# Three block pairs by seven products in the second half of the SSD output projection, and norm roots and inverse denominators spread through DRAM

## Chip, cores, metric

The kernel runs on one core of a Trainium2 chip. The metric is the device time of one execution in microseconds (us). Engines are named as in the profile: PE (TensorE matmul), PEld (its weight loads), DVE (VectorE), ACT (ScalarE), POOL (GpSimd), SP (SyncE, which only issues transfers here).

## The reference

One layer of a hybrid decoder in fp32 on 512 tokens of width 1024. Two branches, dilated window attention and a Mamba-2 scan (SSD), are merged by gates; a gated FFN follows.

```
proj = rmsnorm(h) @ w_in                          # q k v z xBC dt gates
q, k, v, z, xbc, dt, gates = split(proj)
# SSD: 32 heads of 64 in 4 groups, chunks of 128
yg = (scan(silu(conv(xbc)), dt) + d_skip*xh) * silu(z)      # 512 x 2048
yg = yg * rsqrt(mean(yg*yg over each group of 512) + eps)   # one root per token and group
ssm = yg * ssm_norm_w
# attention: 24 heads in 3 dilated groups, 8 outputs of 64
attn = sum over groups of softmax(lse) * o        # the denominators are divided out
merged = g0 * (attn @ w_attn_branch) + g1 * (ssm @ w_ssm_branch)
h = h + merged @ w_out
h = h + (silu(gate) * up) @ w_ffn_out             # gate, up = rmsnorm(h) @ w_ffn_in
out = rmsnorm(h)
```

The change is in `ssm @ w_ssm_branch` (2048 by 1024), in the root of each group, and in the division by the denominators.

## The kernel before

All activations are kept transposed, 128 features on the partitions and 512 tokens along the row. To keep fp32 accuracy each operand of a product is split in two parts, hi (ACT copies it to a rounded type, L81 and L258) and lo (DVE subtracts, L82 and L259), and PE multiplies hi by hi, hi by lo and lo by hi (`mm`, L179). One block of 128 outputs over 1024 inputs is thus 8 x 3 = 24 matmuls of 512 columns (`project`).

`Weights` brings the weight blocks in the order of a plan: SP loads a block of 128x1024 into `wraw` (L65) two blocks ahead, ACT and DVE split it into `whi` and `wlo` one block ahead, in three buffers each. One such ring, `wst`, serves all stages up to the FFN. SP's queue is in order, so a load that waits for a buffer holds all behind it.

The stages, by the profile's clock: norm and first values to about 40 us; the SSD projections and the scan in 16 pairs of heads (four per group) to 374; values of group 1 to 395.6 and of group 2 to 417.4; the second half of the SSD output projection to 461; attention to about 673; gates, merge and `w_out` to about 790; FFN to the end. The first half of the SSD output projection (input tiles 0 to 7) follows the third group. `hook` is called between products and lets the pieces of small work, generators that end each piece with `yield`, advance by one. In the SSD stage and in attention a scheduler sets the order on each engine; in the FFN the order on PE is that of the code.

`group_end` (L601) ends a group: `mean_pow` forms the root `gnr` (128x4: token p of chunk c) on POOL (L273), `spread` turns it with four transposes on PE (`turn`, L182) into a row of 512 tokens on all partitions, ACT copies that to `gnb` (L606), and DVE multiplies four tiles by it (L610), which are then split into `ssmh` and `ssml`. `softmax_pair` ends with the inverse denominators `rd` (L814, L815): POOL widens them to `rdw` (L817), four transposes turn them, DVE multiplies `ot` by the result (L824).

`Pairs` serves the FFN: it takes two 128-row blocks of outputs over two halves of inputs as a 2 by 2 block product and computes it by seven products instead of eight. `fa` and `fb` are the raw loads, `fA`, `fS` and `fD` the split blocks and sums of blocks (`first`, `sums13`, `sums24`, `last`). Each product is 4 x 3 = 12 matmuls of 256 columns, 84 in a pair. There the lo part of `fA` and `fD` is completed by an accumulating transfer that POOL issues (L121). In the diff, `w_ssm[j][:, 8:16]` is the block of weights of output block j and input tiles 8 to 15.

Of the kernel before, what the change touches and what calls it, by code (L numbers as in the profile page):

```python
# [14 lines left out]
P = 128  # L15
S = 512
# [78 lines left out]
class Pairs:  # L95

    def __init__(self, nc, wp, fw, pairs):
        self.nc, self.wp, self.fw, self.pairs = nc, wp, fw, pairs  # L100
        self.raw, self.sums, self.left = {}, {}, {}
# [49 lines left out]
    def sums24(self, n):  # L151
        if n >= len(self.pairs):
            return
        r1, r2 = self.raw[n]
        t = self.fw.tile([P, KD * P], F32, tag="s24", name=f"s24_{n}")
        self.nc.vector.tensor_add(t[:, :S], self.sums.pop(n)[:, :S], r1[:, :S])
# [12 lines left out]
def trunk(ctx: ExitStack, tc: tile.TileContext, xT, w_in, w_v, w_dt, w_attn, w_ssm, w_out, w_fi, w_fo,  # L169
# [40 lines left out]

    wst = Weights(nc, wp, _chunk_plan(w_in, w_v, w_attn, w_ssm, w_out))

# [24 lines left out]

    def project(ps, rhs, first=True, last=True, at=None, w=wst):
        h, l, kt = w.next()
# [12 lines left out]
        return ps  # L252
# [85 lines left out]
    relw = [drm.tile([HEADS, LREL[g]], F32, name=f"relw{g}") for g in range(3)]  # L338
    la_d = drm.tile([NSH, S], F32, name="la_d")
    h1_d = drm.tile([P, KD, S], F32, name="h1_d")  # L340
    v_d = [drm.tile([S, S], F32, name=f"v_d{g}") for g in range(3)]
# [196 lines left out]
    with tc.tile_pool(name="sp", bufs=1, reuse_waits="tile") as sp:  # L538
# [62 lines left out]
        def group_end(g):  # L601
            r = mean_pow(sp, [yg.pop((g, "s"))], 512, 4.0 * EPS, "gn")
            yield
            pb = spread(r)
            rb = sp.tile([P, S], F32, tag="gnb", name=f"gnb{g}")
            act.activation(rb, pb, AF.Copy)  # L606
            yield
# [8 lines left out]

        def ssm_half(j, half):
            ps = project(bank("mm"), [ssm[8 * half + i] for i in range(8)])
            if half == 0:
                sbr[j] = sbrp.tile([P, S], F32, tag=f"sbr{j}", name=f"sbr{j}")  # L620
                act.activation(sbr[j], ps, AF.Copy)
            else:
                ev.tensor_add(sbr[j], sbr[j], ps)

# [23 lines left out]
        for g in range(NG):  # L648
# [29 lines left out]
            if g == 2:  # L678
                for j in range(KD):
                    ssm_half(j, 0)  # L680
        pv = [bank("mm") for _ in range(NCH)]
# [14 lines left out]


    attn = [None] * 4
    mscr = [drm.tile([S, 2], F32, name=f"mscr{i}") for i in range(4)]
    nscr = [drm.tile([S, 2], F32, name=f"nscr{i}") for i in range(4)]  # L700
    dscr = [drm.tile([S, 2], F32, name=f"dscr{i}") for i in range(4)]
    ahl_cm = tc.tile_pool(name="ahl", bufs=1, reuse_waits="tile", side="right")

    with tc.tile_pool(name="ap", bufs=1, reuse_waits="tile") as ap:
# [12 lines left out]
        def softmax_pair(hp, q, k):  # L717
# [97 lines left out]
            ev.reciprocal(rd, rd)  # L815
# [8 lines left out]
            ev.tensor_mul(t, t, pr)  # L824
            dump(f"attn{hp}", t)
            attn[hp] = split(holder["ahl"], t, "at", hp)
            yield

# [4 lines left out]

        nc.sync.dma_start(vt[0], v_t[0])
        nc.sync.dma_start(vt[1], by_class(1))
        pv = [bank("mm") for _ in range(NCH)]

        def stage2(tt):
            if tt % 2 == 0:
                vs[0] = tl([P, 2 * S], "P1", f"vs2_{tt}", 2)  # L840
            act.activation(vs[0][:, (tt % 2) * S : (tt % 2) * S + S], pv[tt], AF.Copy)
            if tt % 2:
                nc.sync.dma_start(v_t[2][:, tt - 1 : tt + 1, :], vs[0].rearrange("p (c d) -> p c d", c=2))

        for c in range(4):
            values(pv, 2, c, xn, stage2)
        nc.sync.dma_start(vt[2], by_class(2))
        for j in range(KD):
            ssm_half(j, 1)
            dump(f"sbr{j}", sbr[j])  # L850
        ssm_cm.__exit__(None, None, None)
        holder["ahl"] = ahl_cm.__enter__()
# [46 lines left out]
        for hp in range(4):  # L899
            q, k = [], []  # L900
            for g in range(3):
                ps = project(bank("mm"), xn)
# [29 lines left out]

    HS = S // 2
    fr_cm = tc.tile_pool(name="fr", bufs=1, reuse_waits="tile", side="right")
# [67 lines left out]
    rb2h = fp.tile([P, S], F32, name="rb2h")  # L1002
    half = [slice(0, HS), slice(HS, S)]

# [199 lines left out]
def _chunk_plan(w_in, w_v, w_attn, w_ssm, w_out):  # L1204
    plan = [w_v[0, c] for c in range(4)]
    for g in range(NG):
# [3 lines left out]
        if g == 2:  # L1210
            plan += [w_ssm[j][:, 0:8] for j in range(KD)]
    plan += [w_v[g, c] for g in (1, 2) for c in range(4)]
    plan += [w_ssm[j][:, 8:16] for j in range(KD)]
    for hp in range(4):
# [3 lines left out]
    for j in range(KD):  # L1218
        plan += [w_in[G0 + j], w_attn[j]]
    return plan + [w_out[j] for j in OUT_ORDER]  # L1220

# [89 lines left out]
```

## Time and profile before

| | |
|---|---|
| runs | 1148.74, 1148.74, 1149.55 us, median 1148.74 |
| profiled execution | 1150.79 us, its span 1149.0 |
| granted clock | 0.996 of full speed |
| busy share | PE 99%, PEld 84%, DVE 62%, ACT 50%, POOL 16% |
| instructions | 17104, of them 6636 matmuls |
| DMA | 142.35 MB, mean 124 GB/s |

The profile shows one execution. A row of a timeline gives the start, the duration, the engine, the line, and what is written from what, with the shape; "x4" puts four following ones together; in brackets stands how long the engine had been idle and what ended that. A row of waits gives total time, times and the longest. A row of groups gives the total and the mean duration of one in nanoseconds. Matmuls overlap, so the mean duration of one is longer than the distance from one to the next. A row of transfers gives count, size of one, and the median time from issue to landing.

### The profile page before, as it was taken

How to read it: one execution, taken by the hardware profiler on the slowest of the kernel's cores; microseconds unless marked ns; L12 is line 12 of the kernel's file. 1: busy time of each engine (PE TensorE's matmuls, PEld its weight loads, DVE VectorE, ACT ScalarE, POOL GpSimd, SP SyncE). 2: the span in 40 equal slices, each digit the busy share in tenths (PEclk: the TensorE clock that was granted, in tenths of full speed). 3: DMA queues.
4: the chain of work that ended last, by engine and by line, in shares of the span. 5: the costliest groups of instructions: out<-in, count | busy, mean ns of one | idle time of the engine just before them, and what ended most of it. 6: DMA issues, size and time to landing. Idle time of an engine off the chain costs nothing.

```text
span 1149.0 us, 17104 instructions
## 1 busy us (share of the span) xinstructions
PE 1132.8 (99%) x6636; PEld 969.5 (84%) x6636; DVE 715.3 (62%) x1253; ACT 569.9 (50%) x997; POOL 181.6 (16%) x169
## 2 busy tenths in 40 slices
PE   9999999999999999999999999999999999999996
PEld 6777888878888788888888888888999999988886
DVE  5777897873579333455564534478888777773222
ACT  5555565554345331336536533356767667663321
POOL 3214313222013300011211100000111111100001
PEclk9999999999999999999999999999999999999999
DMA  6343333233332373332333224345688888844322
GB/s 220 130 149 98 121 94 111 92 111 110 92 92 74 110 256 96 106 93 75 93 85 83 63 90 123 112 151 171 148 184 186 191 193 186 172 129 129 101 65 74
DMA packets 51521, 142.35 MB, mean 124 GB/s; under 512 B 6439, under 2 KB 13119, under 8 KB 51184
## 3 DMA queue, kind: packets, MB, share of 16 engines
q1 hardware_dynamic: 42096, 120.90, 33.9%
q0 software_dynamic: 6896, 16.04, 8.4%
q10 hardware_dynamic: 2448, 4.32, 1.3%
q8 instruction: 52, 0.85, 0.3%
q14 instruction: 29, 0.24, 0.1%
HBM read 133.76 MB, written 7.48 MB: 123 GB/s over the span
## 4 chain that ended last, share of the span: by engine, by line
PE 91%; DVE 4%; DMA 2%; ACT 1%; issue 1%; POOL 0%; SPq 0%; ACTq 0%; DVEq 0%; POOLq 0%
PE mm L179 74%; PE aux L179 15%; PE aux L182 2%; DVE wlo L82 1%; DMA x<-xT 0%; DMA lab<-la_d 0%; DVE frl L950 0%; DMA h_d<-h 0%; ACT whi L81 0%; DVE fS_lo L138 0%; DMA fa<-w_fi 0%; DVE xm L469 0%; DVE h L958 0%; POOL n2r L273 0%; DVE fA_lo L131 0%
## 5 line engine op out<-in xcount | busy, mean ns | idle before, releaser
L82 DVE TENSOR_TENSOR wlo<-wraw,whi 128x1024 fp32r<-128x1024 f32 (+2 forms) x156 | 185.7, 1195 | 185.3 <-ACT whi L81 185.1
L81 ACT ACTIVATE whi<-wraw 128x1024 fp32r<-128x1024 f32 (+2 forms) x156 | 152.2, 981 | 267.1 <-PE mm L179 238.1
L179 PE MATMUL mm<-xnh,whi 128*128 128x512 f32 x640 | 251.8, 393 | 1.4 <-DVE acc L530 1.3
L179 PE MATMUL mm<-xnh,wlo 128*128 128x512 f32 x640 | 252.6, 395 | 0.0
L179 PE MATMUL mm<-xnl,whi 128*128 128x512 f32 x640 | 251.1, 392 | 0.0
L179 PEld LDWEIGHTS mm<-xnh,whi 128*128 128x128 f32 x640 | 120.3, 188 | 27.3 <-ACT ce L562 1.7
L179 PEld LDWEIGHTS mm<-xnh,wlo 128*128 128x128 f32 x640 | 120.2, 188 | 26.9 <-issue 2.7
L179 PEld LDWEIGHTS mm<-xnl,whi 128*128 128x128 f32 x640 | 120.2, 188 | 24.9 <-issue 1.2
L179 PE MATMUL mm<-hhl,whi 128*128 128x512 f32 (+1 forms) x171 | 62.6, 366 | 0.6 <-DVE hhl L259 0.6
L179 PE MATMUL mm<-hhh,whi 128*128 128x512 f32 (+1 forms) x171 | 62.8, 368 | 0.2 <-ACT hhh L258 0.2
L179 PE MATMUL mm<-hhh,wlo 128*128 128x512 f32 (+1 forms) x171 | 62.3, 365 | 0.0
L121 POOL DMA_DIRECT2D fD_lo<-w_fi x22 | 19.1, 866 | 246.3 <-DVE h L958 135.8
L563 POOL TENSOR_TENSOR ce<-ce,Cf 128x768 f32<-128x768 f32 x16 | 34.7, 2173 | 140.9 <-ACT ce L562 78.2
L530 DVE SCALAR_TENSOR_TENSOR acc<-mm,hcw,acc 128x511 f32<-128x511 f32 (+2 forms) x72 | 53.2, 743 | 1.0
L138 DVE TENSOR_TENSOR fS_lo<-s,fS_hi 128x1024 fp32r<-128x1024 f32 x44 | 52.0, 1217 | 0.0
L179 PE MATMUL mm<-ssml,whi 128*128 128x512 f32 x128 | 50.2, 392 | 0.0
L179 PE MATMUL mm<-ssmh,wlo 128*128 128x512 f32 x128 | 50.1, 392 | 0.0
L179 PE MATMUL mm<-ssmh,whi 128*128 128x512 f32 x128 | 49.9, 390 | 0.0
L179 PE MATMUL mm<-frh,fS_hi 128*128 128x256 f32 x176 | 49.4, 281 | 0.5 <-ACT c L1031 0.5
L179 PE MATMUL aux<-frh,fS_hi 128*128 128x256 f32 x176 | 49.4, 280 | 0.0
L179 PE MATMUL aux<-frl,fS_hi 128*128 128x256 f32 x176 | 49.1, 279 | 0.0
L179 PE MATMUL aux<-frh,fS_lo 128*128 128x256 f32 x176 | 49.1, 279 | 0.0
(320 smaller groups left out, 2571.1 us busy)
## 6 DMA issues: line engine op xcount, KB each, us to landing
wraw<-w_in SPq DMA_DIRECT2D x80, 512.0 KB, 3.6
fb<-w_fi SPq DMA_DIRECT2D x22, 512.0 KB, 3.7
fa<-w_fi SPq DMA_DIRECT2D x22, 512.0 KB, 5.0
fA_lo<-w_fi POOLq DMA_DIRECT2D x19, 512.0 KB, 5.8
lab<-la_d SPq DMA_DIRECT2D x16, 512.0 KB, 3.7
wraw<-w_ssm SPq DMA_DIRECT2D x16, 512.0 KB, 3.8
wraw<-w_fo SPq DMA_DIRECT2D x15, 512.0 KB, 3.6
wraw<-w_v SPq DMA_DIRECT2D x11, 512.0 KB, 3.7
```

What stands on the lines that cost most here:

```text
L81: self.nc.scalar.activation(hi[:, cs], r[:, cs], AF.Copy)
L82: self.nc.vector.tensor_sub(lo[:, cs], r[:, cs], hi[:, cs])
L121: self.nc.gpsimd.dma_start(lo.rearrange("p (k n) -> p k n", n=P), src, accum_op=ALU.add)
L138: self.nc.vector.tensor_sub(lo, t, hi)
L179: pe.matmul(out, lhsT, rhs, start=start, stop=stop, skip_group_check=True)
L182: pe.transpose(out, src, ident)
L530: ev.scalar_tensor_tensor(acc[:, d:], ps[:, : S - d], hcw[:, t * 4 + 3 - d : t * 4 + 4 - d], acc[:, d:], op0=ALU.mult, op1=ALU.add)
L563: gp.tensor_mul(ce, ce, Cf[:, P:].unsqueeze(1).to_broadcast([P, 2, S - P]))
```

## The change

Three parts. First, in the second half of the SSD output projection, output blocks 0 and 1 stay as they are, and blocks 2 to 7 are computed as three pairs by `seven`, with the class `Rights` forming the sums of the other factor (`mh`, `ml` in the rows). The sums for the first pair are made beside the values of group 2. The weights of these six blocks leave the ring, which ends there; a second ring `wst2` serves what follows, and its first block comes in eight pieces. The last pair's `fD` is split by ACT and DVE, with no accumulating transfer. Second, the roots of groups 0 to 2 and, third, the inverse denominators are written to DRAM and read back to all partitions. Besides, `hook` is called after each of the four value tiles instead of after every second one, values of group 2 leave in four transfers, and `vt` is loaded in the first attention pair.

```diff
-    def last(self, n):
+    def last(self, n, add=True):
         hi, lo = self.parts(self.wp, "w%s", f"fD{n}")
-        self.added(hi[:, :S], lo[:, :S], self.raw.pop(n)[1][:, S:], self.pairs[n][1][:, 4:8])
+        raw = self.raw.pop(n)[1][:, S:]
+        if add:
+            self.added(hi[:, :S], lo[:, :S], raw, self.pairs[n][1][:, 4:8])
+        else:
+            self.nc.scalar.activation(hi[:, :S], raw, AF.Copy)
+            self.nc.vector.tensor_sub(lo[:, :S], raw, hi[:, :S])
...
             if at is not None:
                 if (c, tt) in at:
                     at[c, tt]()
-            elif tt % 2:
+            else:
                 hook(tt == 3)
...
         def group_end(g):
             r = mean_pow(sp, [yg.pop((g, "s"))], 512, 4.0 * EPS, "gn")
-            yield
-            pb = spread(r)
+            if g < 3:
+                nc.sync.dma_start(gn_d[g].rearrange("(c p) -> p c", p=P), r)
+            yield
             rb = sp.tile([P, S], F32, tag="gnb", name=f"gnb{g}")
-            act.activation(rb, pb, AF.Copy)
+            if g < 3:
+                nc.sync.dma_start(rb, gn_d[g : g + 1, :].partition_broadcast(P)[:, 0, :])
+            else:
+                act.activation(rb, spread(r), AF.Copy)
             yield
...
+    class Rights:
+        def whole(self, i):
+            x = self.pool.tile([P, S], F32, tag="mx", name=f"mx{i}", bufs=3)
+            ev.tensor_add(x, self.tiles[i][0], self.tiles[i][1])
+            self.both = x
+            return [x[:, c] for c in half]
+        def parts(self, p, f, sl):
+            hi, lo = self.own[p]
+            act.activation(hi[:, sl, :], f, AF.Copy)
+            ev.tensor_sub(lo[:, sl, :], f, hi[:, sl, :])
+        def upper(self, p):
...
+        def lower(self, p):
...
+    def seven(pool, fi, x, top, bottom, ahead):
+        for n in range(N):
+            if n == N - 1:
+                ahead()
+            r, q, s_ = bank("mm")[:, :HS], bank()[:, :HS], bank()[:, :HS]
+            add_product(r, fi, n, "a11", x.block(True, 0), True, False)
+            c1 = copied(r, "c1", n)
+            fi.first(n + 1)
+            add_product(q, fi, n, "s1", x.mixed(0), True, False)
+            c5 = copied(q, "c5", n)
+            fi.last(n, n < N - 1)
+            add_product(s_, fi, n, "a12", x.block(False, 0), True, True)
+            top(n, 0, s_, c1)
+            fi.sums13(n + 1)
+            add_product(r, fi, n, "s2", x.mixed(1), False, False)
+            u2 = copied(r, "u2", n)
+            if before:
+                finish(*before)
+            add_product(q, fi, n, "s4", x.block(False, 1), False, True)
+            top(n, 1, q, u2)
+            fi.load(n + 2)
+            fi.sums24(n + 1)
+            add_product(r, fi, n, "s3", x.mixed(3), False, False)
+            bottom(n, 1, r, c5)
+            before = n, r
+        finish(*before)
...
+        fs = Pairs(nc, wp, ts, [(w_ssm[j][:, 8:16], w_ssm[j + 1][:, 8:16]) for j in range(2, KD, 2)], True)
+        xs = Rights(ts, ssm[8:])
+        fs.load(0)
+        for p in range(4):
+            xs.upper(p)
...
+        for c in range(4):
+            values(pv, 2, c, xn, stage2)
...
+        for j in range(2):
+            ps = project(bank("mm"), ssm[8:])
+            ev.tensor_add(sbr[j], sbr[j], ps)
+        drain()
+        del quick[:]
+        main[0] = wst2
+        with tc.manual_schedule(engines={mybir.EngineType.PE}):
+            seven(ts, fs, xs, ssm_top, ssm_bottom, lambda: wst2.fill(1))
...
-            rdw = tl([P, NCH, P], "ot", f"rdw_{hp}", 2)
-            gp.tensor_copy(rdw.rearrange("p b (e d) -> p b e d", e=2), rd.unsqueeze(3).to_broadcast([P, NCH, 2, 64]))
-            pr = bank()
-            for b in range(4):
-                turn(pr[:, b * P : b * P + P], rdw[:, b])
+            for e in range(2):
+                nc.sync.dma_start(rscr[hp][e].rearrange("(b p) -> p b", p=P), rd[:, :, e])
             t = tl([P, S], "ot", f"ot{hp}", 2)
             act.activation(perm(t), regular(o1), AF.Copy)
             ev.tensor_add(t, t, o0)
-            ev.tensor_mul(t, t, pr)
+            yield
+            rdw = tl([P, S], "rdw", f"rdw_{hp}", 1)
+            for e in range(2):
+                nc.sync.dma_start(rdw[halves[e], :], rscr[hp][e : e + 1, :].partition_broadcast(64)[:, 0, :])
+            ev.tensor_mul(t, t, rdw)
```

Where the instructions stand, at three places. On PE, at the start of the third direct block of the projection before, every row is 512 wide:

```order
L179 MATMUL mm_3811<-ssmh_151_3604,wlo_3783 128x512
L179 MATMUL mm_3843<-ssmh_108_2625,whi_3814 128x512
L179 MATMUL mm_3843<-ssml_108_2626,whi_3814 128x512
L179 MATMUL mm_3843<-ssmh_108_2625,wlo_3815 128x512
L179 MATMUL mm_3843<-ssmh_109_2630,whi_3814 128x512
```

In the changed kernel, at the start of the second direct block (`mm_3881`), the narrow rows of the first pair appear (`fA`, `fS` its weights, `mh`, `ml` the sums of the other factor):

```order
L185 MATMUL mm_3881<-ssmh_105_2614,whi_3839 128x512
L185 MATMUL mm_3881<-ssml_105_2615,whi_3839 128x512
L185 MATMUL mm_3909<-ssmh_105_2614,fA_hi 128x256
L185 MATMUL mm_3909<-ssml_105_2615,fA_hi 128x256
L185 MATMUL mm_3909<-ssmh_105_2614,fA_lo 128x256
```

So the pair's first product (and its second, 24 narrow matmuls in all) stands ahead of the rest of the second direct block, whose other 22 wide matmuls follow them.

On DVE, after the root of group 0 before (`a`, `cbm` and `acc` are steps of the next pair of heads, `wlo` a weight split):

```order
L560 TENSOR_TENSOR a_1391<-a_1391,cbm_1245 128x1024
L560 TENSOR_TENSOR a_1528<-a_1528,cbm_1245 128x1024
L82 TENSOR_TENSOR wlo_1511<-wraw_1440,whi_1510 128x1024
L530 SCALAR_TENSOR_TENSOR acc_1427<-mm_1370,hcw,acc_1427 128x511
L530 SCALAR_TENSOR_TENSOR acc_1427<-mm_1370,hcw,acc_1427 128x510
L610 SCALAR_TENSOR_TENSOR yg_801<-yg_801,prm,gnb_1276 128x512
```

and in the changed kernel:

```order
L570 TENSOR_TENSOR a_1388<-a_1388,cbm_1247 128x1024
L570 TENSOR_TENSOR a_1525<-a_1525,cbm_1247 128x1024
L562 TENSOR_TENSOR xw_1386<-xtm_1306,te 128x384
L82 TENSOR_TENSOR wlo_1508<-wraw_1437,whi_1507 128x1024
L624 SCALAR_TENSOR_TENSOR yg_802<-yg_802,prm,gnb_1273 128x512
```

The products with `gnb` stand at nearly the same place; the two `acc` went behind them and `xw` came ahead.

On SP before, at the root of group 0, only weight loads follow one another:

```order
L65 DMA wraw_1508<-w_in 128x1024
L65 DMA wraw_1577<-w_in 128x1024
L65 DMA wraw_1646<-w_in 128x1024
L65 DMA wraw_1715<-w_in 128x1024
L65 DMA wraw_1784<-w_in 128x1024
```

and in the changed kernel:

```order
L65 DMA wraw_1505<-w_in 128x1024
L65 DMA wraw_1574<-w_in 128x1024
L614 DMA gn_d<-gnr_1235 128x4x1
L618 DMA gnb_1273<-gn_d 128x512
L65 DMA wraw_1643<-w_in 128x1024
```

The write of the root, which waits for POOL, and the read, which waits for the write to land, stand ahead of the third weight load.

More of the change, by code (lines that the diff above doesn't have):

```diff
@@ L209, in par @@
         return prm[:, a + i : a + i + w]
-    wst = Weights(nc, wp, _chunk_plan(w_in, w_v, w_attn, w_ssm, w_out))
+    plan, rest = _chunk_plan(w_in, w_v, w_attn, w_ssm, w_out)
+    wst = Weights(nc, wp, plan)
+    wst2 = Weights(nc, wp, rest)
+    main = [wst]
     late, quick, slow = [], [], []
@@ L236, in drain, with project @@
             hook(True)
-    def project(ps, rhs, first=True, last=True, at=None, w=wst):
-        h, l, kt = w.next()
+    def project(ps, rhs, first=True, last=True, at=None, w=None):
+        h, l, kt = (w or main[0]).next()
         for k in range(kt):
@@ L339, in trunk @@
     la_d = drm.tile([NSH, S], F32, name="la_d")
+    gn_d = drm.tile([3, S], F32, name="gn_d")
     h1_d = drm.tile([P, KD, S], F32, name="h1_d")
@@ L615, in group_end, with ssm_half @@
                     yield
[L617 to L623, printed above, removed]
+        def ssm_half(j):
+            ps = project(bank("mm"), ssm[:8])
+            sbr[j] = sbrp.tile([P, S], F32, tag=f"sbr{j}", name=f"sbr{j}")
+            act.activation(sbr[j], ps, AF.Copy)
         def transposed(src, tag, bufs, name, t=None):
@@ new lines, in seven, with copied, finish @@
+    def seven(pool, fi, x, top, bottom, ahead):
+        def copied(ps, tag, n):
+            t = pool.tile([P, HS], F32, tag=tag, name=f"{tag}_{n}", bufs=1)
+            act.activation(t, ps, AF.Copy)
+            return t
+        def finish(n, r):
+            add_product(r, fi, n, "a22", x.mixed(2), False, True)
+            bottom(n, 0, r, None)
+        N = len(fi.pairs)
+        before = None
+        for n in range(N):
[23 more added lines that the diff above has]
+        finish(*before)
@@ new lines, in trunk, with lowers, stage2, ssm_top @@
+    with tc.tile_pool(name="ts", bufs=1, reuse_waits="tile") as ts:
+        fs = Pairs(nc, wp, ts, [(w_ssm[j][:, 8:16], w_ssm[j + 1][:, 8:16]) for j in range(2, KD, 2)], True)
+        xs = Rights(ts, ssm[8:])
+        fs.load(0)
+        for p in range(4):
+            xs.upper(p)
+        fs.first(0, add=False)
+        fs.sums13(0)
+        fs.sums24(0)
+        def lowers():
+            for p in range(4):
+                for _ in range(4):
+                    yield
+                xs.lower(p)
+            fs.load(1)
+        quick.append([lowers()])
+        pv = [bank("mm") for _ in range(NCH)]
+        def stage2(tt):
+            t = ts.tile([P, S], F32, tag="vs", name=f"vs2_{tt}", bufs=2)
+            act.activation(t, pv[tt], AF.Copy)
+            nc.sync.dma_start(v_t[2][:, tt, :], t)
+        for c in range(4):
+            values(pv, 2, c, xn, stage2)
+        def ssm_top(n, h, ps, c):
+            o = sbr[2 * n + 2][:, half[h]]
+            ev.tensor_add(o, o, c)
+            ev.tensor_add(o, o, ps)
+        def ssm_bottom(n, h, ps, c):
+            o = sbr[2 * n + 3][:, half[h]]
+            if c is not None:
+                ev.tensor_sub(o, o, c)
+            ev.tensor_sub(o, o, ps)
+        for j in range(2):
[6 more added lines that the diff above has]
+            seven(ts, fs, xs, ssm_top, ssm_bottom, lambda: wst2.fill(1))
+        for j in range(KD):
+            dump(f"sbr{j}", sbr[j])
@@ L698, in trunk @@
+    ssm_cm.__exit__(None, None, None)
     attn = [None] * 4
@@ L700, in trunk @@
     nscr = [drm.tile([S, 2], F32, name=f"nscr{i}") for i in range(4)]
+    rscr = [drm.tile([2, S], F32, name=f"rscr{i}") for i in range(4)]
     dscr = [drm.tile([S, 2], F32, name=f"dscr{i}") for i in range(4)]
@@ L1211, in _chunk_plan @@
             plan += [w_ssm[j][:, 0:8] for j in range(KD)]
-    plan += [w_v[g, c] for g in (1, 2) for c in range(4)]
-    plan += [w_ssm[j][:, 8:16] for j in range(KD)]
+    head = plan + [w_v[g, c] for g in (1, 2) for c in range(4)] + [w_ssm[j][:, 8:16] for j in range(2)]
+    plan = []
     for hp in range(4):
```

66 lines of the change are left out of this document (42 added, 24 removed).

## The prediction

> **What bounds the kernel now.** I read the page first, for the engine that is never idle and for the chain that ended last.
>
> ```profile
> span 1149.0 us, 17104 instructions
> ...
> PE 1132.8 (99%) x6636; PEld 969.5 (84%) x6636; DVE 715.3 (62%) x1253; ACT 569.9 (50%) x997; POOL 181.6 (16%) x169
> ...
> PEclk9999999999999999999999999999999999999999
> ...
> PE 91%; DVE 4%; DMA 2%; ACT 1%; issue 1%; POOL 0%; SPq 0%; ACTq 0%; DVEq 0%; POOLq 0%
> ```
>
> TensorE (PE) is busy for 99% of the span at full granted clock, and the chain runs through it for 91%. So time goes where TensorE work goes, unless another engine makes it wait. The waits of PE say how little there is to win besides (columns: total us, times, longest).
>
> ```profile
> PE aux L179 <- ACT sq L1173: 1.4, 1, 1.4
> PE mm L179 <- DVE acc L530: 1.3, 1, 1.3
> ...
> PE mm L179 <- ACT c L1031: 0.5, 1, 0.5
> ```
>
> The largest single wait is 1.4 us. A copy of a product (c, L1031) delays PE once by 0.5 us in all 22 pairs of the FFN, which already multiply by seven products. Next come two stretches by engine: the second half of the SSD projection as it is, and two FFN pairs.
>
> ```profile
> core 0: us, PE busy (x) PEld busy (x) DVE busy (x) ACT busy (x) POOL busy (x), PEclk, DMA share, GB/s
> ...
> 417.40:461.00 43.60, 43.60 (x195) 36.08 (x194) 14.62 (x15) 9.01 (x10) 1.04 (x2) 1.00 0.45 155
> 809.30:829.10 19.80, 19.80 (x170) 19.80 (x169) 17.36 (x30) 14.77 (x24) 3.49 (x4) 1.00 0.78 183
> ```
>
> In the projection VectorE (DVE) works 14.62 of 43.60 us, in FFN pairs 17.36 of 19.80 with PE still full. The pattern that the change brings in is thus one that PE can run without waiting, but with a loaded DVE.
>
> **The pairs.** Durations of overlapping matmuls are not their pitch, so I take the pitch from two unbroken pieces of the chain (start, us, what).
>
> ```profile
> 398.79 96.37 PE mm L179 x425
> ...
> 809.35 2.83 PE mm L179 x24
> ```
>
> 96.37/425 = 0.2268 us for a 512-wide matmul, 2.83/24 = 0.1179 us for a 256-wide one. Six of the eight output blocks leave: 6 x 24 = 144 wide matmuls, 144 x 0.2268 = 32.65 us. In their place stand three pairs with 84 narrow ones each: 252 x 0.1179 = 29.71 us. The gain is 2.94 us. The 108 additional weight loads are in the narrow pitch already, since the FFN window has PEld busy for all its 19.80 us.
>
> A rule of the Trainium skill speaks against this step: in *TensorE: Matmul & The Clock Gate*, section "Back-to-back issue gap", a sustained stream is given 81 ns at 128 columns and 131 ns at 512. An estimate on a straight line between these gives 98 ns at 256, so 252 x 0.098 - 144 x 0.131 = 24.7 - 18.9, a loss of 5.8 us instead of the gain of 2.94. The trace does not agree with it: its wide pitch is 227 ns, near the 216 ns that the same section calls the isolated gap.
>
> The pairs' DVE and ACT work lies beside PE work: the sums for pair 0 beside the values of group 2 and the two direct blocks, those of pairs 1 and 2 beside the pair before, as in the FFN window. Their loads (fa, fb and the accumulating POOL transfers) meet a DMA share of 0.45 where the FFN lives with 0.78. The last pair's fD goes through ACT and DVE, so no POOL transfer has to land at its end. The first weights for attention come in eight pieces, asked for one whole pair (84 x 0.1179 = 9.9 us) ahead; with a landing of 3.7 us (lab, below) that is covered; without the cover it would cost those 3.7 us. I take all of this at nothing; what it costs if DVE falls behind is the second rival.
>
> **The turns.** Three of the four norm spreads (four transposes each) and all four of the denominators (four each) leave PE. Their price is the step from the start of the turns to the start of what follows.
>
> ```profile
> 147.50 0.60 PE L182 MATMUL aux<-ident,gnr 128*128 128x128 f32 x4
> 147.94 0.60 PE L182 MATMUL aux<-ident,xf 128*128 128x128 f32 x4
> ...
> 582.80 0.66 PE L182 MATMUL aux<-ident,rdw 128*128 128x128 f32 x4
> 583.22 0.47 PE L179 MATMUL mm<-xnh,whi 128*128 128x512 f32 x1
> ```
>
> That is 0.44 and 0.42 us, so 3 x 0.44 + 4 x 0.42 = 3.00 us. ACT's gnb copy and POOL's rdw copy go as well; neither ended a PE wait, so they are worth nothing.
>
> **The norm trips.** In the place of the spreads SP writes the roots to DRAM and, when that has landed, reads 128x512 back. No such trip is in the trace; these rows bound it (KB of one, median us from issue to landing).
>
> ```profile
> lab<-la_d SPq DMA_DIRECT2D x16, 512.0 KB, 3.7
> x<-xT SPq DMA_DIRECT2D x8, 256.0 KB, 6.0
> wraw<-w_attn SPq DMA_DIRECT2D x8, 256.0 KB, 2.6
> ...
> mscr<-m POOLq DMA_DIRECT2D x4, 4.0 KB, 4.6
> dscr<-d POOLq DMA_DIRECT2D x4, 4.0 KB, 1.7
> ```
>
> The write is 2 KB in 512 scattered elements; mscr and dscr are small writes of 4 KB and give 1.7 to 4.6. I take 2.5, nearer to the shorter, since it is half their bytes. The read is 256 KB: 2.6 (w_attn) to 6.0 (x, eight loads at the kernel's start). I take 3.0, between w_attn with the same bytes and lab with twice those. Around them stand two issues by SP, 0.33 us each in the row below, and three hand-overs between engines, for which I put 0.1 each: 0.96 in all, so 6.5 us from the root to VectorE.
>
> ```profile
> 140.88 0.33 SPq L65 DMA_DIRECT2D wraw<-w_in  x1
> ...
> 142.22 1.04 POOL L273 TENSOR_TENSOR gnr<-gnv,mhalf 128x4 f32<-128x4 f32 x1 [3.56 <-DVE gnv L271]
> ...
> 143.65 2.36 DVE L560 TENSOR_TENSOR a<-a,cbm 128x1024 f32<-128x1024 f32 x2
> 145.93 1.22 DVE L82 TENSOR_TENSOR wlo<-wraw,whi 128x1024 fp32r<-128x1024 f32 x1
> ...
> 148.14 0.60 ACT L606 ACTIVATE gnb<-aux 128x512 f32<-128x512 f32 x1 [2.11 <-PE aux L182]
> ...
> 160.13 0.46 DVE L573 SCALAR_TENSOR_TENSOR S<-S,eE,aux 128x64 f32<-128x64 f32 x2
> ...
> 162.38 0.83 PE L179 MATMUL aux<-ce,S 128*64 128x128 f32 x12
> ...
> 216.99 0.75 DVE L530 SCALAR_TENSOR_TENSOR acc<-mm,hcw,acc 128x509 f32<-128x509 f32 x1
> ...
> 217.10 1.02 POOL L273 TENSOR_TENSOR gnr<-gnv,mhalf 128x4 f32<-128x4 f32 x1 [3.72 <-DVE gnv L271]
> ...
> 226.43 0.55 DVE L552 TENSOR_TENSOR xw<-xtm,te 128x384 f32<-128x384 f32 x1
> ...
> 282.78 1.02 POOL L273 TENSOR_TENSOR gnr<-gnv,mhalf 128x4 f32<-128x4 f32 x1 [5.51 <-DVE gnv L271]
> ...
> 289.38 2.74 DVE L610 SCALAR_TENSOR_TENSOR yg<-yg,prm,gnb 128x512 f32<-128x512 f32 x4 [1.47 <-ACT gnb L606]
> ```
>
> Group 0: the root is there at 143.26, so the row at 149.8. In the new order VectorE has the two a, an xw and a wlo ahead of the four products with gnb. The two a take 2.36 and the next starts 2.28 after their start, so commands lap by 0.08, and VectorE is at the products at 145.93 + 0.47 + 1.14 = 147.5. It idles 2.3 us. Behind the products stand, in its queue, the state updates S and later weight splits; S ends at 160.59 and PE takes it up at 162.38, a lead of 1.8, so 0.5 us would reach PE. Group 1: root at 218.1, row at 224.6; three acc, cbm, two a and xw stand ahead, 5.6 us from 216.99, which is 222.6. Idle 2.0, and by the same lead 0.2. Group 2: root at 283.8, row at 290.3 against products that start at 289.38 now, behind an idle 1.47; what follows there are weight splits, for which VectorE has that idle time: nothing. Sum 0.7 us. The lower end is nothing (VectorE's earlier idle time is then spent waiting), the upper, at 4.6 and 6.0, is the third rival. A gain beyond the turns isn't excluded: the SSD stage has waits like the 1.3 us for acc above, and the change also lets a step of the pair work run at every value tile, so that VectorE may be earlier there.
>
> On SP the write is ahead of weight loads, and while it lands they cannot be issued.
>
> ```profile
> SPq L65 <- DVE wlo L82: 642.2, 135, 14.3
> ```
>
> SP waits for a weight buffer 642.2/135 = 4.8 us a time. A hold of 0.33 + 2.5 us fits in that; at 4.6 it just does not. I take nothing.
>
> By the Trainium skill, *DMA: Bandwidth & Descriptors*, "Rules for kernel authors", a strided last dimension lowers to one descriptor per element, and by "Anatomy of one DMA" a transfer costs about 2.0 us and its bytes at 436 GB/s; an estimate of the trip from that page is 2.0 + 2.6, with issues and hand-overs 5.6 us instead of 6.5, and the sum would be without the 0.7. Nothing in this trace shows what 512 descriptors add.
>
> **The denominator trips.**
>
> ```profile
> 569.20 0.20 DVE L815 RECIPROCAL rd<-rd 128x8 f32<-128x8 f32 x1
> ...
> 584.84 0.69 DVE L824 TENSOR_TENSOR ot<-ot,aux 128x512 f32<-128x512 f32 x1
> ```
>
> From the reciprocal to the product that uses it pass 15.4 us. The trip of two writes, a read, a weight load and a second read takes about 6.5 + 3 x 0.33 = 7.5 us, at the upper ends 12.6. So it is covered, and the one command behind, the split of the attention result, isn't multiplied until the merge. SP's weight loads stand behind the write for 3 us, as above. Nothing. The three vt loads (twice lab's bytes each, so about 3 x 7.4 = 22 us by that row) now stand in the first attention pair, the last of them behind its first four projections; the attention starts at 461.0 and vt is first multiplied at 534.5:
>
> ```profile
> L179 PE MATMUL aux<-P,vt x192: 272/273/430, 534.5 to 672.3; 128*64 128x128 f32 x144, 128*64 128x256 f32 x48
> ```
>
> 461 + 4 x 24 x 0.2268 + 22 = 505 at the latest, so nothing again.
>
> **Sum.** -2.94 - 3.00 + 0.7 = -5.2 us. Against the profiled execution's own 1150.79 us (span 1149.0 and 1.8 around it) that is 1145.6. The median of the runs, 1148.74, is 2.05 below that execution; the same difference taken from it gives 1143.5 us. What a measurement of this kernel can tell from no change is about 0.2%, or 2.3 us: faster means below 1146.4.
>
> **Rivals.** *First, the forecast*, 1143.5; its own range is 1141.5 (1148.74 - 5.94 = 1142.8, less the 1.3 us of the acc wait) to 1145.4.
>
> *Second, VectorE is late at the first pair.* It needs the groups of sums before PE does, on top of the last group's products and splits, whose place is kept:
>
> ```profile
> L1082 DVE TENSOR_TENSOR g<-aux,c 128x256 f32<-128x256 f32 x22 | 9.2, 416 | 2.0 <-PE aux L179 2.0
> ...
> L623 DVE TENSOR_TENSOR sbr<-sbr,mm 128x512 f32<-128x512 f32 x8 | 5.5, 688 | 26.1 <-PE mm L179 26.1
> ```
>
> ```profile
> 399.46 2.74 DVE L610 SCALAR_TENSOR_TENSOR yg<-yg,prm,gnb 128x512 f32<-128x512 f32 x4 [1.21 <-ACT gnb L606]
> ```
>
> From those products to the last quarter of pair 0's s3 product, the new order has 62 VectorE commands: 28 of 512 columns, 27 of 256 and 7 of 1024. At full length they take 28 x 0.688 + 27 x 0.416 + 7 x 1.22 (the wlo row above) = 39.0 us, lapped by 0.08 each 34.0. PE meanwhile has the rest of the values (399.46 to 417.4, where the projection's window starts, 17.9), two direct blocks (48 x 0.2268 = 10.9), five products of 12 (5 x 1.415) and three quarters of one (1.06): 37.0 us. So VectorE is 3.0 early when lapped and 2.0 late when not; if it also waits for three ACT copies of 0.60 us (the gnb row above) it is 3.8 late. Price 2.0 to 3.8 us, time 1145.5 to 1147.3. For it speaks that a hi part must come from ACT before each subtraction; against it that the FFN window runs VectorE at 17.36 of 19.80 us with PE full.
>
> *Third, on the other side: the norm trips are slow.* A write of 4.6 and a read of 6.0 bring group 0's row at 143.26 + 0.96 + 10.6 = 154.8, 7.3 after VectorE is there, and group 1's at 229.7, 7.1 after. Less 1.8 each, that is 5.5 + 5.3 = 10.8 us on PE, and 1148.74 - 5.94 + 10.8 = 1153.6. It decides from the point where the two waits take back 5.94, that is 1.8 + 2.97 = 4.8 us of idle per group, write and read together 8.2. For it speak 512 scattered elements, of which this trace has no like; against it that the rows of 6.0 come from the crowded start.
>
> *Fourth, the pairs save nothing.* If a narrow matmul can't go under 144/252 = 0.571 of a wide one, or the 21 products each wait 2.94/21 = 0.14 us at their start, the sum is -3.00 + 0.7 and the time 1146.4. Against it stand 0.1179/0.2268 = 0.520 and the 0.5 us of waits for copies in 22 pairs. The skill's sustained figures above would take it further, to 1152 as an estimate; with the trace's pitch they have no chance of their own.
>
> **Chances.** Forecast 0.64, second 0.18, third 0.08, fourth 0.10. Faster by over 0.2% are the forecast, half of the second and half of the fourth: 0.78. Within it are the other halves and a little of the third: 0.15. Slower is the third: 0.07. The likeliest gives 1143.5; the range goes from 1141.0 (the forecast's low end with half a microsecond for the spread of the runs) to 1147.6 (all of the second, and the fourth, with 0.3 for the same), which leaves out the third and some 0.06 of tails.
>
> **What would show it.** Of the changed kernel's profile: the turns L182 fewer by 28; PE's pieces of the three pairs at 1.415 us per twelve; VectorE's idle time ahead of the gnb products about 2 us in groups 0 and 1; the landing of gn_d and gnb near 2.5 and 3.0; no PE wait for S, xf, wlo, or for the fS parts in the first pair. A PE wait for S or wlo after 150 or 225 us, or landings whose sum passes 8.2, make the third rival right; one for fS or m parts inside the first pair the second. I would be wrong beyond these if the planner's order, which moves much besides, puts a new PE wait in the SSD stage.

## The result, and the profile after

The changed kernel takes 1155.95 us (median of 11 runs, 1149.21 to 1158.61) where the kernel before takes 1148.74. The ratio is 1.0054, with a 95% interval of 1.0038 to 1.0071: slower by 0.54%, some 6 us, where 5.2 us less were forecast. The third rival, slow norm trips, came true, and beyond the 1153.6 us that it was given.

The page of the changed kernel (profiled execution 1151.97 us; the lines of the span, of the busy times and of the chain):

```profile
span 1150.1 us, 17443 instructions
...
PE 1125.6 (98%) x6716; PEld 967.4 (84%) x6716; DVE 746.4 (65%) x1325; ACT 585.8 (51%) x1036; POOL 180.2 (16%) x169
...
PE 85%; DVE 7%; DMA 4%; issue 2%; ACT 2%; POOL 1%; SPq 0%; ACTq 0%; POOLq 0%; DVEq 0%
PE mm L185 67%; PE aux L185 16%; PE aux L188 2%; DVE wlo L82 2%; DMA gn_d<-gnr 2%; DVE acc L540 1%; ACT whi L81 1%; DMA gnb<-gn_d 1%; DVE frl L1096 1%; DVE a L568 0%; DMA x<-xT 0%; DVE yg L624 0%; DMA h_d<-h 0%; DMA lab<-la_d 0%; DMA fa<-w_fi 0%
```

TensorE is busy for 7.2 us less than before (1125.6 against 1132.8), yet the span is longer. The chain that ended last runs through TensorE for 85% instead of 91%: the write `gn_d` and its read `gnb` now stand on it. Some places of the chain after the first root (start, us, what):

```profile
142.56 1.05 POOL gnr L282
143.61 0.02 issue
143.62 8.86 DMA gn_d<-gnr
152.49 0.02 issue
152.50 4.28 DMA gnb<-gn_d
156.78 0.03 issue
156.81 2.74 DVE yg L624 x4
```

The write took 8.86 us to land, where 2.5 were put and 4.6 was the upper end; the read 4.28, where 3.0 were put. What that did, in the waits (total us, times, longest) of TensorE and of VectorE:

```profile
PE aux L188 <- DVE xf L545: 5.1, 1, 5.1
PE mm L185 <- DVE acc L540: 3.8, 2, 3.3
```

```profile
DVE yg L624 <- DMA gnb<-gn_d: 27.3, 3, 9.6
```

VectorE stood still three times, 27.3 us in all, in front of the four products. `xf` and `acc` are queued behind them, and TensorE waits for those, 3.3 us in group 0 and 5.1 us in group 1. Group 2's wait, the longest, is one that TensorE never feels. And there was a cost that the prediction has nowhere. Windows of 10 us around the two waits (us, busy of PE, PEld, DVE, ACT, POOL with counts, PE clock, DMA share, GB/s), and the first matmuls behind the first wait:

```profile
160.00:170.00 10.00, 6.74 (x25) 5.09 (x24) 9.96 (x18) 4.86 (x8) 0.00 (x0) 0.83 0.35 104
240.00:250.00 10.00, 8.32 (x44) 6.46 (x45) 10.00 (x23) 5.00 (x14) 0.00 (x0) 0.66 0.34 107
```

```profile
165.60 0.47 PE L185 MATMUL mm<-xnh,whi 128*128 128x512 f32 x1 [3.26 <-DVE acc L540]
165.90 0.59 PE L185 MATMUL mm<-xnl,whi 128*128 128x512 f32 x1
166.29 0.63 PE L185 MATMUL mm<-xnh,wlo 128*128 128x512 f32 x1
166.72 0.63 PE L185 MATMUL mm<-xnh,whi 128*128 128x512 f32 x1
```

From the third to the fourth of these matmuls it is 0.43 us instead of the usual 0.227: after the pause the clock is granted at half speed for a while. In the windows that is 10 x (1 - 0.83) = 1.7 us lost behind the first wait and 10 x (1 - 0.66) = 3.4 at the second, of which 0.3 fall into the pause itself, so that 3.1 cost time. So the two trips cost 3.3 + 1.7 and 5.1 + 3.1, 13.2 us, against 5.94 of removed TensorE work and one older wait less (acc, 1.3 in the trace before): 1148.74 - 5.94 - 0.8 + 13.2 = 1155.2, if I put the older wait's part at 0.8 (0.5 of it is still in the 3.8 for acc). The median is 1155.95.

The profiled execution is 4.0 us below that median, and it differs from the one before in two places that the change doesn't touch. One is the FFN. A piece of its chain, before and after (start, us, what):

```profile
863.07 2.83 PE mm L179 x24
```

```profile
864.95 2.72 PE mm L185 x24
```

2.72/24 = 0.1133 us per narrow matmul here, 0.1179 before; over 22 x 84 matmuls that would be 8.5 us. From its first to its last matmul the FFN takes 221.6 us here and 229.0 before, so 7.4. All the other kernels below were profiled at 0.118 us, so this execution's FFN is the odd one; the trace's span must not be compared with 1149.0 without it. The other place is the start. The first matmuls of the projections and of the FFN, before and after (ns, first and last start in us):

```profile
L179 PE MATMUL mm<-xnh,whi x640: 387/389/504, 39.1 to 745.8; 128*128 128x512 f32 x160
L179 PE MATMUL mm<-frh,fA_hi x88: 279/280/387, 787.8 to 1003.9; 128*128 128x256 f32 x88
```

```profile
L185 PE MATMUL mm<-xnh,whi x640: 387/390/629, 40.2 to 753.6; 128*128 128x512 f32 x160
L185 PE MATMUL mm<-frh,fA_hi x88: 275/277/388, 795.5 to 1004.5; 128*128 128x256 f32 x88
```

The projections begin 1.1 us later, and the FFN 795.5 - 787.8 = 7.7 us later. Trace against trace the sum makes 1.1 - 5.94 - 0.8 + 13.2 = 7.6, so the account holds up to the FFN.

### The profile page after: what moved, and what is told of

It is laid out like the page before. It is cut to its first block, busy times and chain, and to the rows that moved or that the text cites. A ratio compares the mean times of both kernels' runs of the same rounds, so it can differ in the third digit from the quotient of the medians.

```text
span 1150.1 us, 17443 instructions
## 1 busy us (share of the span) xinstructions
PE 1125.6 (98%) x6716; PEld 967.4 (84%) x6716; DVE 746.4 (65%) x1325; ACT 585.8 (51%) x1036; POOL 180.2 (16%) x169
## 4 chain that ended last, share of the span: by engine, by line
PE 85%; DVE 7%; DMA 4%; issue 2%; ACT 2%; POOL 1%; SPq 0%; ACTq 0%; POOLq 0%; DVEq 0%
PE mm L185 67%; PE aux L185 16%; PE aux L188 2%; DVE wlo L82 2%; DMA gn_d<-gnr 2%; DVE acc L540 1%; ACT whi L81 1%; DMA gnb<-gn_d 1%; DVE frl L1096 1%; DVE a L568 0%; DMA x<-xT 0%; DVE yg L624 0%; DMA h_d<-h 0%; DMA lab<-la_d 0%; DMA fa<-w_fi 0%
## 5 line engine op out<-in xcount | busy, mean ns | idle before, releaser
L82 DVE TENSOR_TENSOR wlo<-wraw,whi 128x1024 fp32r<-128x1024 f32 (+3 forms) x157 | 178.6, 1146 | 156.7 <-ACT whi L81 156.6
L81 ACT ACTIVATE whi<-wraw 128x1024 fp32r<-128x1024 f32 (+3 forms) x157 | 146.2, 941 | 214.6 <-PE mm L185 187.7
L138 DVE TENSOR_TENSOR fS_lo<-s,fS_hi 128x1024 fp32r<-128x1024 f32 x50 | 59.4, 1218 | 2.2 <-ACT fS_hi L137 2.2
L137 ACT ACTIVATE fS_hi<-s 128x1024 fp32r<-128x1024 f32 x50 | 51.0, 1048 | 9.4 <-DVE s L148 4.9
L185 PE MATMUL mm<-frl,fS_hi 128*128 128x256 f32 x176 | 48.7, 277 | 0.0
L185 PE MATMUL mm<-frh,fS_lo 128*128 128x256 f32 x176 | 48.7, 277 | 0.0
```

What stands on the lines that cost most here:

```text
L81: self.nc.scalar.activation(hi[:, cs], r[:, cs], AF.Copy)
L82: self.nc.vector.tensor_sub(lo[:, cs], r[:, cs], hi[:, cs])
L137: self.nc.scalar.activation(hi, t, AF.Copy)
L138: self.nc.vector.tensor_sub(lo, t, hi)
L185: pe.matmul(out, lhsT, rhs, start=start, stop=stop, skip_group_check=True)
```

## The experiments

Two theories at first. Theory 1: the trips of the roots cost the time, and the pairs and the denominators bring what was forecast. Theory 2: the pairs cost it, by VectorE's additional work or the new order. In the diffs "..." stands for lines left out. Ratios are to the kernel before, run on the same chip, with 95% intervals; microseconds are the ratio's share of 1149.

**pairs_only.** All four spreads and the denominators by transposes again; the hook at every value tile and the later vt loads stay.

```diff
+            pb = spread(r)
-                nc.sync.dma_start(gn_d[g].rearrange("(c p) -> p c", p=P), r)
...
+            for b in range(4):
+                turn(pr[:, b * P : b * P + P], rdw[:, b])
```

> The changed kernel with all four norm spreads and the denominators by transposes again: only the three pairs by seven products (with the hook at every value tile and the later vt loads) are left of the change. Theory 1 (the trips of the norm roots through DRAM cost the time): 2.9 us less than before, 1145.8, no new PE wait in the SSD stage, clock at 1.00 from 40 to 373 us. Theory 2 (the pairs cost it, by VectorE's added work or by the new order): 1150 or more, with PE waits at the first pair or for xf and S.

0.9974 (0.9964 to 0.9985), 3.0 us less (1.7 to 4.1). In the window from values of group 2 to the end of the pairs TensorE is never idle:

```profile
373.80:461.00 87.20, 87.20 (x524) 76.59 (x523) 58.99 (x108) 41.83 (x73) 9.71 (x10) 1.00 0.45 133
```

VectorE works 58.99 of 87.20 us there (30.5 in the kernel before) without making TensorE wait. Theory 2 falls.

**turned_roots.** The change with the roots by transposes; pairs and denominator trips stay.

> The changed kernel with the roots of all four groups by transposes again; pairs and denominator trips stay. Theory 1: 1148.7 - 2.9 - 1.7 = 1144.1, the waits for xf (5.1) and acc (3.3) and the half-clock windows behind them are gone. Theory 2: 1149 or more. If the denominator trips cost something, it is above pairs_only instead of 1.7 below it.

0.9964 (0.9950 to 0.9977), 4.1 us less (2.6 to 5.7). No wait for xf, S or acc above 0.4 us. One edit, the roots, takes 10 us back.

**roots_only.** The kernel before, with the diff of `group_end` alone.

> The kernel before with only the roots of groups 0 to 2 through DRAM. Theory 1: 1.3 us less for twelve transposes, 8.4 us more of PE waits and 3 to 5 us more for the windows at half clock behind them: 1158 to 1161, the write landing in about 9 us. Theory 2: 1147.4, nothing but the transposes.

1.0094 (1.0076 to 1.0112), 10.8 us more (8.7 to 12.9), inside what theory 1 expects (median 1159.92). The waits of TensorE and the landings are near those of the changed kernel:

```profile
PE aux L182 <- DVE xf L536: 4.1, 1, 4.1
PE mm L179 <- DVE acc L531: 3.3, 1, 3.3
```

```profile
gn_d<-gnr SPq DMA_DIRECT2D x3, 2.0 KB, 8.8
```

Trace against trace the account closes here too: the turns and the older wait for acc, 1.3 us each, are gone, the waits add 4.1 + 3.3, the half clock behind them 1.7 + 1.6, and the start 0.2, 8.3 us in all; the first matmul of the FFN starts at 796.1 against 787.8.

**denoms_only.** The kernel before, with the diff of `softmax_pair` alone.

> The kernel before with only the denominators through DRAM. Theory 1: sixteen transposes less, -1.7 us, 1147.0, since the trips (two writes that land in 9 us, two reads in 5) end before their product and nobody waits behind it. Rival: SP's queue stands for 9 us four times, weight loads come late and it is as before or slower, 1149 or more.

0.9991 (0.9975 to 1.0008): 1.0 us less, between 2.9 less and 0.9 more. The forecast 1.7 less is inside, and so is no change; a loss of more than 0.9 is not. The writes are as slow as the roots'. VectorE waits a little for the result, and TensorE not at all (transfers: KB of one, median landing; waits):

```profile
rscr<-rd SPq DMA_DIRECT2D x8, 2.0 KB, 9.0
```

```profile
DVE ot L826 <- DMA rdw<-rscr: 2.3, 2, 1.5
```

The three parts alone give -3.0 - 1.0 + 10.8 = +6.8 us; together they gave +6.2.

**behind_splits.** Is it the long trip, the loads that SP holds behind it, or only VectorE's place in its queue? The slow write stays; the products of groups 0 and 1 are put behind a later weight split (`wst.last` is the latest subtraction for a `wlo`).

```diff
-            yield
+            for _ in range(1 if g > 1 else 12):
+                yield
+            behind = wst.last.ins
...
+                    with tc.issue_after(behind):
+                        ev.scalar_tensor_tensor(y, y, par("nsw", t), rb, ...)
```

> The changed kernel, its slow scattered write kept, with the four products of groups 0 and 1 held on VectorE behind a weight split about two blocks later. Theory 1, that only VectorE's standing still in front of the products costs time: trip as long as before (write about 9 us, read about 4), no wait of VectorE for gnb over 2 us in groups 0 and 1, no PE wait for xf or acc, the clock whole, and 1148.7 - 2.9 - 3.0 = 1142.8, at most 1146. Rival, that SP's weight loads held behind the write for 9 us cost it: PE waits for weight parts (whi or wlo), 1150 or more.

1143.03 us, 0.9950 (0.9934 to 0.9967): 5.7 us less (3.8 to 7.6), where 5.94 were worked out for TensorE alone. The write is as slow as ever, VectorE waits for one row only, group 2's, and the windows that had lost clock are whole:

```profile
gn_d<-gnr SPq DMA_DIRECT2D x3, 2.0 KB, 8.7
```

```profile
DVE yg L628 <- DMA gnb<-gn_d: 10.0, 1, 10.0
```

```profile
160.00:170.00 10.00, 10.00 (x48) 8.36 (x47) 10.00 (x19) 5.43 (x8) 2.28 (x1) 1.00 0.31 105
240.00:250.00 10.00, 10.00 (x68) 8.26 (x67) 9.02 (x20) 5.38 (x14) 0.43 (x1) 1.00 0.35 121
```

So the trip and SP's hold cost little or nothing (the interval's lower end, 3.8, leaves room for 2 us); what costs is the place of the waiting commands in VectorE's queue. This version beats both kernels. In its trace the FFN begins 9.5 us earlier than before (778.3), of which 2.9 come from the start (36.2 against 39.1) and are not the change's.

**rows_of_four.** Why is the write slow? The roots are written as they lie, 128 runs of 16 bytes, and put in order by the access pattern of the products.

```diff
-                nc.sync.dma_start(gn_d[g].rearrange("(c p) -> p c", p=P), r)
+                nc.sync.dma_start(gn_d[g].rearrange("(p c) -> p c", p=P), r)
...
-                ev.scalar_tensor_tensor(y, y, par("nsw", t), rb, ...)
+                ev.scalar_tensor_tensor(view(y), view(y), par("nsw", t), rb.rearrange("p (q c) -> p c q", c=NCH), ...)
```

> The changed kernel with the roots written as they lie, four neighbouring values per partition (128 runs of 16 bytes instead of 512 scattered values of 4), read back as one row, and the order put right by VectorE's access pattern in the products. If the scattered values make the write slow: it lands in 2 to 3 us, the trip takes 7 to 8, VectorE idles 3 us instead of 9, PE waits 0 to 1 us, time 1143 to 1146. If any write to DRAM from SP lands in 9 us: 1156 as the changed kernel.

1145.55 us, 0.9970 (0.9957 to 0.9983): 3.4 us less (2.0 to 4.9). The same 2 KB land in 2.0 us (2.0, 3.5 and 1.5), and TensorE waits for S 1.7 us and for xf 0.4, where it was 8.4 for xf and acc:

```profile
gn_d<-gnr SPq DMA_DIRECT2D x3, 2.0 KB, 2.0
```

```profile
PE aux L185 <- DVE S L583: 1.7, 2, 1.2
```

**rows_behind and rows_behind_2.** Both mends together, the products one and two blocks later.

> Runs of 16 bytes and the products of groups 0 and 1 behind a split one block later, both together. Theory 1: the waits that rows_of_four had left (0.4 for xf and 1.2 for S, 1.6 us in all) are gone: 1143 to 1144.5, about 1.5 below rows_of_four. Rival: the trip is free already and nothing moves beside rows_of_four (0.997).

> rows_behind with the products two blocks later instead of one, so in VectorE's order of behind_splits, with the products through the access pattern (1.14 us each instead of 0.75). If the order was what spoiled rows_behind (its wait for S, 1.8 us): 1143 to 1144.5 as behind_splits. If the slower products were: four times 0.4 us in each of two groups on VectorE, 1146 to 1149.

rows_behind missed: 1148.52 us, 0.9998 (0.9979 to 1.0017). TensorE waits for S once for 1.8 us, and there too the clock falls behind it (a window of 6 us with 0.72 of it, 1.7 us lost):

```profile
PE aux L185 <- DVE S L583: 2.2, 2, 1.8
```

```profile
186.00:192.00 6.00, 6.00 (x21) 4.07 (x21) 3.96 (x13) 3.61 (x5) 1.29 (x1) 0.72 0.51 167
```

rows_behind_2, in the order of behind_splits, has no such wait: 1144.61 us, 0.9957 (0.9934 to 0.9980). The difference of the medians, 3.9 us, is near those 1.8 + 1.7, which speaks for the order as what spoiled rows_behind; the two were measured on different chips, and their intervals just touch. The access pattern isn't free either: in rows_behind a product takes 1142 ns (busy us, mean ns), the plain one of group 3 745:

```profile
L629 DVE SCALAR_TENSOR_TENSOR yg<-yg,prm,gnb 128x512 f32<-128x512 f32 x12 | 12.9, 1142 | 3.6 <-DMA gnb<-gn_d 3.6
L631 DVE SCALAR_TENSOR_TENSOR yg<-yg,prm,gnb 128x512 f32<-128x512 f32 x4 | 2.7, 745 | 1.0 <-ACT gnb L620 1.0
```

**The write by itself.** Three kernels with additional writes that nobody waits for. In the first they stand where the queues are busy, which settles little:

> The kernel before with eight additional writes to DRAM in the gates' stage, which nobody waits for: on SP 512 scattered values of 4 bytes, 128 runs of 16 bytes, 128 values of 4 bytes, 256 scattered values, one run of 2 KB, 1024 scattered values; and the 512 scattered values once on ACT's queue and once on POOL's. If the number of runs sets the landing: 512 values 9 us, 256 about 5.5, 1024 about 16, 128 about 3 whatever their size, one run 2; ACT's queue as SP's. If it is the scattering or the number of bytes: 128 values of 4 bytes differ from 128 runs of 16 bytes.

There (1164.29 us in all, for its additional transfers) 128 values of 4 bytes land in 7.7 us, 256 in 8.7, 512 in 9.6 on SP, 14.5 on ACT's queue and 13.7 on POOL's, and 1024 in 15.2. The 128 runs of 16 bytes took 9.6 too, but that write only began to move some 7 us after its issue, behind other transfers; the one run of 2 KB has no landing in the trace. The other two put one write at each root of turned_roots, where the queue is free:

```diff
+            if g == 0:
+                nc.sync.dma_start(out[:P].rearrange("(p c) -> p c", c=1), r[:, :1])
+            elif g == 1:
+                nc.sync.dma_start(out[: 2 * P].rearrange("(p c) -> p c", c=2), r[:, :2])
+            elif g == 2:
+                nc.sync.dma_start(out[: 2 * P].rearrange("(c p) -> p c", p=P), r[:, :2])
```

> The kernel turned_roots with one more write at the end of groups 0 to 2, at the place where the changed kernel writes its roots, which nobody waits for and nobody reads: 128 values of 4 bytes, 128 runs of 8 bytes, 256 scattered values of 4 bytes. Measured so far at this place: 512 scattered values 8.7 to 9.1 us, 128 runs of 16 bytes 1.5 to 3.9. If the number of pieces sets the landing (about 0.018 us apiece above 128): 2, 2 and 4.5 us. If it is that a piece has only 4 bytes: 128 values take 5 us or more, against 2 for 128 runs of 8 bytes.

> As probe_roots_a with 32 runs of 8 bytes, 32 values of 4 bytes, and the 512 scattered values from ACT's queue. If the number of pieces sets the landing: 2, 2, and 9 us. If 4-byte pieces are slow as such: 2, 5 or more, 9. If SP's queue is the slow part, the last lands in 3 to 5.

Transfers in windows around the three roots of probe_roots_a (128 values of 4 bytes; 128 runs of 8; 256 values of 4), and of probe_roots_b (32 runs of 8; 32 values of 4; 512 values from ACT); one execution each, 1143.94 and 1142.70 us:

```profile
gn_d<-gnr SPq DMA_DIRECT2D x1, 0.5 KB, 8.0
...
gn_d<-gnr SPq DMA_DIRECT2D x1, 1.0 KB, 2.8
...
gn_d<-gnr SPq DMA_DIRECT2D x1, 1.0 KB, 8.1
```

```profile
gn_d<-gnr SPq DMA_DIRECT2D x1, 0.2 KB, 3.2
...
gn_d<-gnr SPq DMA_DIRECT2D x1, 0.1 KB, 3.1
...
gn_d<-gnr ACTq DMA_DIRECT2D x1, 2.0 KB, 9.3
```

With 128 pieces it is the size of the piece that decides: 4 bytes 8.0 us, 8 bytes 2.8, 16 bytes 1.4 to 3.5 (nine writes of the three rows_ kernels; the 3.9 in the expectation is a read). From 128 on the number does not: 128, 256 and 512 pieces of 4 bytes take 8.0, 8.1 and 8.8. Only 32 of them are quick (3.1), which neither theory of the expectation had. The queue isn't the cause (ACT 9.3). Apart from the runs of 16 bytes and the 512 values, each of these is a single write; why 128 pieces of 4 bytes are slow and 32 are not stays open.

## Why the prediction was wrong, step by step

- **The pairs, -2.94:** right; 3.0 measured, together with the moves of the change that pairs_only keeps. Their matmuls run at 2.88/24 = 0.1200 us in the changed kernel's chain, not at the FFN's 0.1179, which makes 2.4 by the same working, also inside the interval.
- **The second rival, VectorE late at the first pair:** wrong. TensorE waits there for nothing of the pair, in any of these kernels.
- **The turns, -3.00:** not separated by itself, but behind_splits has all of the gains and comes out at -5.7 for -5.94 forecast.
- **The denominator trips at nothing:** right for TensorE, although their writes took 9 us as well. The 15.4 us of cover were all but enough: VectorE waited twice, 1.5 us at most in denoms_only.
- **SP's hold at nothing:** right within the 2 us said above, and with a hold of 9 us, not 3: behind_splits shows it.
- **The norm trips, +0.7: here it failed**, at the sentence "I take 2.5, nearer to the shorter, since it is half their bytes". The bytes are not what the landing follows. The rows that bounded the write were the wrong kin, since the prediction took them by their 4 KB and did not ask in what pieces they go: by the code, dscr's 1.7 us are for 128 runs of 32 bytes and mscr's 4.6 for 512 runs of 8, both from POOL's queue, while the roots go in 512 pieces of 4 and took 8.86 in group 0. The read, put at 3.0, took 4.28. By the prediction's own break-even, write and read together 8.2, the real 13.1 decides against the change. The prediction had one descriptor per element before it, said that nothing in the trace shows what 512 of them add, and left them to the third rival at 0.08. Its estimate from the Trainium skill, *DMA: Bandwidth & Descriptors*, section "Anatomy of one DMA", put the write at 2.0 us; that section gives the figure for transfers that GpSimd issues, and this one SP issued.
- **The issues and hand-overs, 0.96, were too much.** In the chain only 0.02 + 0.02 + 0.03 us stand between root, write, read and product; the landings counted from the issue hold the rest, and no run shows the 0.1 put for each hand-over. With the real landings the prediction's working gives 143.26 + 0.96 + 13.1 - 147.5 = 9.8 us of idle for VectorE in group 0; 8.86 were measured, and the 0.9 between them is this term.
- **The lead of 1.8 us was too small.** Of 8.86 and 8.85 us of VectorE's idle, 3.26 and 5.14 reached TensorE, so the lead was 5.6 and 3.7, in the new order where TensorE first missed acc and xf, not S. That error helped the change.
- **The clock behind a wait was left out:** 4.8 of the 13.2 us. The prediction priced a wait at its length. That the third rival's 1153.6 lies near the 1155.95 is luck: a longer trip and the clock were made up for by a longer lead.

By the Trainium skill, *TensorE: Matmul & The Clock Gate*, section "Why this matters for your kernels", gaps of TensorE should stay under some 3 us, because one window of idle brings the clock back to half. The trace agrees for 3.26 and 5.14 us (1.7 and 3.1 us lost), but rows_behind lost its 1.7 us behind a wait of 1.8 us, so here a shorter wait was enough. The prediction drew on the same page and left this rule out.

## What to carry to other kernels

Before a value takes a trip through DRAM, count the pieces and their bytes, not the bytes of the whole: 128 or more pieces of 4 bytes landed in 8 to 10 us where the queue was free, the same values in runs of 16 bytes in 1.4 to 3.5. A long trip costs nothing as long as no in-order queue stands still in front of its result: move the consumer, not the producer, until what is queued behind it is in time. And a wait of the bounding engine costs more than its length where the clock falls behind it; here 13.2 us for 8.4.

## What the hardware showed that I had not expected

- A write of 512 scattered values lands 8.2 to 10.0 us after its issue (nine such writes, in the changed kernel, roots_only and behind_splits), although in the changed kernel the last of its packets is recorded 1.3 and 1.8 us after the issue in two of the three roots, and 3.6 in the third. What the rest of the time goes to is not shown.
- After a pause of 1.8 to 5.1 us the granted clock is 0.5 for 3.4 or 6.8 us: twice in the changed kernel, twice in roots_only, once in rows_behind. The wait of 1.3 us that the kernel before has for acc left no such trace.
- The granted clock changes only on a grid. In the changed kernel's records it is at full for 44 and then for 21 steps of 3.41 us between the drops. Here are the steps at the second wait in the changed kernel, and in roots_only (columns as in the windows above):

```profile
237.61:241.02 3.41, 0.00 (x0) 0.00 (x0) 3.41 (x6) 3.08 (x6) 0.00 (x0) 1.00 0.00 0
241.02:244.43 3.41, 2.75 (x20) 2.46 (x22) 3.41 (x6) 2.84 (x10) 0.00 (x0) 0.50 0.45 159
244.43:247.84 3.41, 3.41 (x17) 2.57 (x14) 3.41 (x9) 0.12 (x1) 0.00 (x0) 0.50 0.21 41
247.84:251.25 3.41, 3.41 (x18) 2.43 (x17) 3.41 (x12) 2.27 (x4) 0.07 (x1) 1.00 0.32 115
```

```profile
236.15:239.56 3.41, 0.58 (x6) 0.44 (x6) 3.41 (x6) 3.32 (x6) 0.00 (x0) 1.00 0.09 20
239.56:242.97 3.41, 3.26 (x26) 2.53 (x25) 3.41 (x7) 1.75 (x8) 0.00 (x0) 0.50 0.36 138
242.97:246.38 3.41, 3.41 (x17) 2.46 (x18) 3.41 (x11) 1.09 (x2) 0.00 (x0) 1.00 0.45 153
```

The pause of 5.14 us reached 0.66 us into the step behind its idle one, and a second step at half followed; the 4.1 us of roots_only reached 0.15 us into it, and one step was all. In all 13 traces, from the first recorded change of the clock on, a step at full clock in which TensorE stood idle for 1.6 us or more was followed by one at half, and a step with 1.2 us or less was not; between them both occur. So what a wait costs depends on where it falls on the grid. This is read off the traces afterwards, and no run was made to test it.

- The start, the same code in all 13 kernels, takes between 36.2 us (behind_splits) and 41.4 (turned_roots) to the first matmul of the projections; the granted clock in the first 20 us is 1.00 in the one and 0.83 in the other.
- The FFN's narrow matmuls ran at 0.1133 us apart in one execution and at 0.1179 in all others profiled, with the same code; 7.4 us hang on it. Single runs some 8 us below their kernel's median (1140.71 of the kernel before, 1138.33 of turned_roots) would fit such an execution, but no trace of one was kept. What sets it is open.
